# State mixer of an encoder: B and C tables stored as [group, channel], scan products and cross sum through PSUM

## The chip, the cores and the metric

The kernel runs on one core of one Trainium2 chip. The metric is device time in microseconds (us). Engines: TensorE (PE; its weight loads PEld), VectorE (DVE), ScalarE (ACT), GpSimd (POOL), SyncE (SP, which issues most DMAs). L498 is line 498 of the kernel before.

## The reference

Two layers over 1040 tokens of width 1024 (16 learned tokens and 1024 inputs). Layer 0 mixes tokens with a bidirectional diagonal complex state space, layer 1 with attention; after each comes a dense SwiGLU layer, and every sub-layer ends in a layer norm. Only the state mixer is touched. Cut to what matters, one direction of it is:

```
abr, abi = exp(lam * dt)                       # one complex factor for each of 64 groups x 64 states
bu  = einsum('blgc,gpc->blgp', u, Bbar)        # 16 channels of a group into 64 complex states
s_t = a * s_{t-1} + bu_t                       # along the 1040 tokens, forwards or in reverse
y   = einsum('blgp,gcp->blgc', Re s, c_re) - einsum('blgp,gcp->blgc', Im s, c_im)
```

The mixer adds both directions and d * u, applies GELU and a gate, and multiplies by an output matrix.

## The kernel before

The tokens are cut into 130 chunks (NK) of T = 8. Partitions 0 to 63 hold the 64 states of the forward direction, 64 to 127 those of the backward one, which is stored in reverse order of the chunks. The state mixer (`s5_phase`) has these stages; each engine takes its instructions in the order in which the code issues them.

Tables. `param_T` transposes the raw B and C parameters on TensorE, four channels to a PSUM bank, and ScalarE copies each bank into a table (L206). The table is laid out as [channel, re or im, group]: for a fixed group, channels lie 128 numbers apart, and 64 apart in the sums Hs and Cs.

G batches (`g_batch`, `x_batch`, 16 batches of four groups). VectorE multiplies B by powers of the factor: three products that read the tables (L335 to L337) and two sums of tiles just made (L338, L339); the k tiles are two deep. TensorE transposes the results (two banks), ScalarE copies them to W (L345), and TensorE multiplies them by the inputs U (four banks), which ScalarE copies into XS, the state of every chunk (L357). Batches 2 to 9 also take part of the input layout with them (one bank, L183 and L191). Beside this GpSimd makes power tables for C (`out_side`).

Scan (L478 to L503). 128 steps, one chunk each, all on VectorE. A step works on two halves of the 64 groups with six instructions: two products with the factor into TA (L494, 128 columns; the factor SB lies in PSUM), two sums of TA and the next chunk (L496, 64 columns), two cross sums (L498, 64 columns) that write the next state.

Written out by hand into the scan's loop stand other engines' instructions, at fixed steps: GpSimd's `e_batch` (five products or sums that make E from C, L386 to L390; the first four or five are issued before the scan), and for every batch `inside`: GpSimd's small dI (L424, L442, L443), TensorE's products of B and E (L433), ScalarE copies to Z (L439 to L441), eight DMAs from Z into M0 (L449), TensorE's products of M0 and U in two banks (L455), ScalarE copies back to U (L460). From step 66 on, `swap` turns the backward half of XS round, piece by piece: a copy to a PSUM bank (L467), and after the matching step two copies back (L470, L471).

Output. For all groups TensorE multiplies E by XS (L521), VectorE adds U (L523), and DMAs carry the result out. Then the gate and the dense layers follow. Just before L521, `late` starts the weight loads and conversions of the gate.

PSUM has eight banks; `bank()` hands out those of the pool `s5_ps` in turn, so a tile waits for the last user of the tile seven allocations before it.

Of the kernel before, what the change touches and what calls it, by code (L numbers as in the profile page):

```python
# [9 lines left out]
FP32 = mybir.dt.float32  # L10
# [3 lines left out]
ALU = mybir.AluOpType  # L14
PSUM = bass.MemoryType.PSUM
# [4 lines left out]
G = 64  # L20
# [5 lines left out]
CH = 16  # L26
T = 8
# [3 lines left out]
def bc(ap, dim, n):  # L31

    a = ap.unsqueeze(dim)
    shape = list(a.shape)
    shape[dim] = n
    return a.to_broadcast(shape)
# [77 lines left out]
def s5_phase(nc, tc, P, a, ident, acc, xres, ydram, late):  # L114

    V, A, PE, PO = nc.vector, nc.scalar, nc.tensor, nc.gpsimd
    ps = P("s5_ps", bufs=7, space=PSUM)

    psc = P("s5_psc", space=PSUM)

    def bank(name="b"):
        return ps.tile([128, 512], FP32, tag="b", name=name)

    def transpose(out, x):
        n = x.shape[0]
        PE.transpose(out, x, ident[:n, :n])

    U = Uv(acc)
    tab = P("s5_tab")
    tab2 = P("s5_tab2")  # L130
# [43 lines left out]
    for k in range(2):  # L174
        nc.sync.dma_start(out=XT[64 * k:64 * k + 64],
                          in_=a["x"][0, 1008 + T * k:1008 + T * k + T, :].rearrange("t (g c) -> g t c", c=CH))
# [16 lines left out]
    def x_tail():  # L193
        b = bank()
        transpose(b[:, :128], XT.rearrange("p t c -> p (t c)"))
        A.copy(out=U[:, :, 128:130], in_=b[:, :128].rearrange("p (k g) -> p g k", k=2))

    def param_T(x, raw):

        PT = tab.tile([128, CH, 2, G], FP32, name=x + "T")  # L200
        for h in range(4):
            b = bank()
            for c4 in range(4):
                c = 4 * h + c4
                transpose(b[:, c4 * 128:c4 * 128 + 128], raw[:, c::CH] if x == "b" else raw[:, c * 128:c * 128 + 128])
            A.copy(out=PT[:, 4 * h:4 * h + 4], in_=b.rearrange("p (c i g) -> p c i g", c=4, g=G))  # L206
        return PT[:, :, 0], PT[:, :, 1]

    load_x(2)
    raw_c = load_param("c")  # L210
# [37 lines left out]
        x_main(p, XG0[:, 4 * p:4 * p + 4])  # L248
    Br, Bi = param_T("b", raw_b)
    x_tail()  # L250
    Hs = tab2.tile([128, CH, G], FP32, name="Hs")
    PO.tensor_tensor(out=Hs, in0=Br, in1=Bi, op=ALU.add)
    AC = pc.tile([64, 4, 128], FP32, name="AC")
    cm, nr, sh, sn, t1, t2, rden = (t[n] for n in ("cm", "nr", "sh", "sn", "t1", "t2", "rden"))
# [17 lines left out]
    b = bank()  # L272
# [38 lines left out]
    Cr, Ci = param_T("c", raw_c)  # L311
    dsk = tab.tile([CH, G], FP32, name="dsk")
    b = bank()
    transpose(b[:CH, :G], dsr)
    A.copy(out=dsk, in_=b[:CH, :G])
    Cs = tab.tile([128, CH, G], FP32, name="Cs")

    SB = psc.tile([128, 512], FP32, name="SB")[:, :256].rearrange("p (j c g) -> p j c g", j=2, g=G)
    A.copy(out=SB[:, 0], in_=bc(PW[:, 0, 8], 1, 2))
    A.copy(out=SB[:, 1, 0], in_=PW[:, 1, 8])  # L320
    A.mul(SB[:, 1, 1], PW[:, 1, 8], -1.0)

# [6 lines left out]
    def g_batch(gb):  # L329
        gs = slice(NB * gb, NB * gb + NB)  # L330
        shp = [128, NB, T, CH]
        q_r, q_s, q_d = (bc(q[:, :, gs].rearrange("p s g -> p g s"), 3, CH) for q in G3)
        h_r, h_i, h_s = (bc(h[:, :, gs].rearrange("p c g -> p g c"), 2, T) for h in (Br, Bi, Hs))
        k1, k2, k3 = (gp.tile(shp, FP32, tag=f"k{i}", name=f"k{i}") for i in range(3))
        V.tensor_tensor(out=k1, in0=h_s, in1=q_r, op=ALU.mult)  # L335
        V.tensor_tensor(out=k2, in0=h_i, in1=q_s, op=ALU.mult)
        V.tensor_tensor(out=k3, in0=h_r, in1=q_d, op=ALU.mult)  # L337
        V.tensor_tensor(out=k2, in0=k1, in1=k2, op=ALU.subtract)  # L338
        V.tensor_tensor(out=k3, in0=k1, in1=k3, op=ALU.add)  # L339
        W = gp.tile([128, NB, 2, 128], FP32, tag="W", name="W")  # L340
        for c2, src in enumerate((k2, k3)):
            b = bank()
            for j in range(NB):
                transpose(b[:, j * 128:(j + 1) * 128], src[:, j].rearrange("p s c -> p (s c)"))
            A.copy(out=W[:, :, c2, :], in_=b.rearrange("p (g m) -> p g m", g=NB))  # L345
        return W
# [32 lines left out]
    def e_batch(gb):  # L379

        gs = slice(NB * gb, NB * gb + NB)
        g0 = NB * gb % (G // 2)
        q_r, q_s, q_d = (bc(q[:, :, gs].rearrange("p s g -> p g s"), 3, CH) for q in E3)
        c_r, c_i, c_s = (bc(c[:, :, gs].rearrange("p c g -> p g c"), 2, T) for c in (Cr, Ci, Cs))
        er, ei = (Eh[2 * gb // NG][:, i, g0:g0 + NB] for i in range(2))
        PO.tensor_tensor(out=ek, in0=c_s, in1=q_r, op=ALU.mult)  # L386
        PO.tensor_tensor(out=er, in0=c_i, in1=q_s, op=ALU.mult)
        PO.tensor_tensor(out=er, in0=ek, in1=er, op=ALU.subtract)
        PO.tensor_tensor(out=ei, in0=c_r, in1=q_d, op=ALU.mult)
        PO.tensor_tensor(out=ei, in0=ei, in1=ek, op=ALU.subtract)  # L390
# [3 lines left out]
    for gb in range(NG):  # L394
        p = 8 + gb - X_AT
# [20 lines left out]

    Eh[1] = P("s5_e1", side="right").tile([128, 2, G // 2, T, CH], FP32, name="E1")
    rp = P("s5_r")
    TA = rp.tile([128, 2, 2, 2, G // 2], FP32, name="TA")
    def inside(gb):  # L420

        gs = slice(NB * gb, NB * gb + NB)
        dI = rp.tile([CH, NB, CH], FP32, tag="dI", name="dI")
        PO.tensor_tensor(out=dI, in0=bc(ident[:CH, :CH], 1, NB), in1=bc(dsk[:, gs], 2, CH), op=ALU.mult)  # L424
        yield 2

        b = bank()
        for j in range(NB):
            g = NB * gb + j
            for c2, src in enumerate((Br, Bi)):  # L430
                for d in range(2):
                    r = slice(64 * d, 64 * d + 64)
                    PE.matmul(b[32 * d:32 * d + CH, j * 128:(j + 1) * 128], src[r, :, g],  # L433
                              E(c2, g)[r].rearrange("p s c -> p (s c)"), start=(c2 == 0), stop=(c2 == 1))
        yield 6
        Z = rp.tile([CH, NB, 2 * T - 1, CH], FP32, tag="Z", name="Z", bufs=2)
        bv = b[:64].rearrange("p (g s c) -> p g s c", g=NB, s=T)
        f0 = rp.tile([CH, NB, CH], FP32, tag="f0", name="f0")
        A.copy(out=f0, in_=bv[0:16, :, 0, :])  # L439
        A.copy(out=Z[:, :, 0:T, :], in_=bv[32:48])  # L440
        A.copy(out=Z[:, :, T:, :], in_=bv[0:16, :, 1:T, :])  # L441
        PO.tensor_tensor(out=dI, in0=dI, in1=f0, op=ALU.add)  # L442
        PO.tensor_tensor(out=Z[:, :, T - 1, :], in0=Z[:, :, T - 1, :], in1=dI, op=ALU.add)  # L443
        yield 8
        M0 = rp.tile([128, NB, 128], FP32, tag="M0", name="M0", bufs=2)
        Zf = Z.rearrange("p g s c -> p g (s c)")
        for t in range(T):
            o = (T - 1 - t) * CH
            nc.sync.dma_start(out=M0[CH * t:CH * t + CH], in_=Zf[:, :, o:o + 128])  # L449
        yield Y_AT  # L450
        banks = []
        for j0 in range(0, NB, 2):
            b = bank()
            for j in range(2):
                PE.matmul(b[:, j * NK:(j + 1) * NK], M0[:, j0 + j], U[:, NB * gb + j0 + j, :], start=True, stop=True)  # L455
            banks.append(b)
        yield Y_AT + 3
        for j0, b in zip(range(0, NB, 2), banks):
            g = NB * gb + j0
            A.copy(out=U[:, g:g + 2, :], in_=b[:, :2 * NK].rearrange("p (g k) -> p g k", g=2))  # L460
# [17 lines left out]
    for i in range(2, NK):  # L478
        for gb in range(NG):
            if i == 2 + int(E_PACE * (gb - EARLY)):  # L480
                e_batch(gb)
            l0 = 3 + int(L_PACE * gb)
            if i == l0:
                work[gb] = [inside(gb), l0]
        for gb in list(work):
            if i >= work[gb][1]:
                at = next(work[gb][0], None)
                if at is None:
                    del work[gb]
                else:  # L490
                    work[gb][1] = 3 + int(L_PACE * gb) + at
        st, nx = XS[:, i - 1], XS[:, i]
        for h, gs in enumerate(halves):
            V.tensor_tensor(out=TA[:, h], in0=SB[:, :, :, gs], in1=bc(st[:, :, gs], 1, 2), op=ALU.mult)  # L494
        for h, gs in enumerate(halves):
            V.tensor_tensor(out=TA[:, h, 0], in0=TA[:, h, 0], in1=nx[:, :, gs], op=ALU.add)  # L496
        for h, gs in enumerate(halves):
            V.tensor_tensor(out=nx[:, :, gs], in0=TA[:, h, 0], in1=TA[:, h, 1, ::-1], op=ALU.add)  # L498
        if sw and len(begun) < 2 and i > NK // 2:
            begun.append((sw[0][0], swap(*sw.pop(0))))  # L500
            next(begun[-1][1])
        while begun and NK - 1 - begun[0][0] <= i - 1:
            next(begun.pop(0)[1], None)  # L503
# [11 lines left out]
    for ft in range(KT):  # L515
        for g0 in range(8 * ft, 8 * ft + 8, 2):
            b = bank()
            for j in range(2):
                g = g0 + j
                for c2 in range(2):  # L520
# [3 lines left out]
                            in1=b[:, :2 * NK].rearrange("p (g k) -> p g k", g=2), op=ALU.add)  # L524
# [1052 lines left out]
```

## Time and profile before

| | us |
|---|---|
| median of 3 runs (lowest to highest) | 2938.03 (2931.74 to 2938.48) |
| the profiled execution | 2936.13 |
| its span | 2934.4 |
| TensorE busy in the span | 2656.4 (91%) |
| VectorE busy | 1651.7 (56%) |
| ScalarE busy | 1153.1 (39%) |
| GpSimd busy | 584.0 (20%) |

The shares are means over stages with different limits: in the page's 40 slices TensorE is at 5, 5, 4, 3 and 6 tenths in the first five (about 73 us each) and at 8 or more in nearly all the rest. So the state mixer is read by windows, and by the order of time of each engine. A row of the timeline has the start, the length, the engine, the line, the operation and the tiles; "x2" means two instructions of a kind in one row, whose length is that of both. A new VectorE instruction starts before the record of the one before it ends, so the distance of starts tells what an instruction takes of the engine.

### The profile page before, as it was taken

The page shows a single profiled execution, that of the slowest core. Times are in us where ns is not written, and L with a number is a line of the kernel's source. Part 1 is how long each engine was busy: PE and PEld are TensorE (multiplying, and loading weights), DVE is VectorE, ACT ScalarE, POOL GpSimd, SP SyncE. Part 2 cuts the span into 40 slices and gives each one's busy share as a digit, 9 for nine tenths or more (in the row PEclk, how much of TensorE's full clock was granted, in tenths as well). Part 3 has the DMA queues.
Part 4 walks back from the last instruction along what each step waited for, and adds up shares of the span by engine and source line. Part 5 has one row for each costly group of instructions (what it writes and reads, how often), then busy time and mean ns, then how long its engine had stood idle before and what let it go on. Part 6 is the DMA issues. An engine that isn't in the chain of part 4 may idle for free.

```text
span 2934.4 us, 43407 instructions
## 1 busy us (share of the span) xinstructions
PE 2656.4 (91%) x17277; PEld 2551.9 (87%) x17277; DVE 1651.7 (56%) x3270; ACT 1153.1 (39%) x2138; POOL 584.0 (20%) x544
## 2 busy tenths in 40 slices
PE   5543689999999999998998998999999999999997
PEld 4432689999999999997997887888999999999996
DVE  8999545573333333337867888887364333333334
ACT  5523353432222112125557777776332121211215
POOL 3983023230000000004204343432230000000002
PEclk8865799999999999998999999999999999999998
DMA  5110375221111111111301121111111111111101
GB/s 120 27 37 16 90 228 177 72 90 63 50 49 46 44 44 44 44 44 58 102 15 37 23 48 27 45 23 60 50 42 52 51 44 51 44 51 44 44 30 58
DMA packets 124837, 167.42 MB, mean 57 GB/s; under 512 B 13499, under 2 KB 104971, under 8 KB 124635
## 3 DMA queue, kind: packets, MB, share of 16 engines
q1 hardware_dynamic: 118203, 141.22, 17.0%
q0 software_dynamic: 5712, 21.30, 2.1%
q8 instruction: 136, 2.23, 0.3%
q10 hardware_dynamic: 720, 2.13, 0.2%
q14 instruction: 66, 0.54, 0.1%
HBM read 126.41 MB, written 21.23 MB: 50 GB/s over the span
## 4 chain that ended last, share of the span: by engine, by line
PE 74%; DVE 16%; ACT 3%; issue 3%; DMA 2%; POOL 1%; SPq 0%; ACTq 0%; DVEq 0%; POOLq 0%
PE bk L682 21%; PE bk L683 21%; PE bk L684 21%; PE pv L1094 4%; PE pt L1072 3%; DVE XS L498 3%; DVE TA L496 3%; DVE mx L1052 3%; DVE pl L1085 2%; PE b L521 2%; DVE TA L494 2%; ACT ph L1080 1%; ACT P L1056 1%; DVE acc L738 1%; PE bk L904 1%
## 5 line engine op out<-in xcount | busy, mean ns | idle before, releaser
L682 PE MATMUL bk<-Hh,unit 128*128 128x348 f32 (+1 forms) x2928 | 956.3, 327 | 9.8 <-ACT Hh L772 6.2
L683 PE MATMUL bk<-Hl,unit 128*128 128x348 f32 (+1 forms) x2928 | 945.4, 323 | 1.1 <-DVE Hl L776 1.0
L684 PE MATMUL bk<-Hh,unit 128*128 128x348 f32 (+1 forms) x2928 | 943.8, 322 | 0.0
L682 PEld LDWEIGHTS bk<-Hh,unit 128*128 128x128 f32 x2928 | 555.2, 190 | 15.1 <-ACT Hh L772 5.8
L683 PEld LDWEIGHTS bk<-Hl,unit 128*128 128x128 f32 x2928 | 554.9, 190 | 6.3 <-DVE Hl L776 2.0
L684 PEld LDWEIGHTS bk<-Hh,unit 128*128 128x128 f32 x2928 | 554.8, 189 | 0.0
L846 DVE TENSOR_TENSOR sg<-sg,bk 128x348 f32<-128x348 f32 x132 | 68.1, 516 | 631.3 <-PE bk L684 623.5
L711 POOL TENSOR_TENSOR lns<-lns,lnsq 128x348 f32<-128x348 f32 (+1 forms) x72 | 70.0, 981 | 1552.2 <-ACT lnsq L709 1551.1
L682 PE MATMUL bk<-gt,unit 128*128 128x348 f32 (+1 forms) x1056 | 340.3, 322 | 0.0
L684 PE MATMUL bk<-gt,unit 128*128 128x348 f32 (+1 forms) x1056 | 338.9, 321 | 0.0
L683 PE MATMUL bk<-gt,unit 128*128 128x348 f32 (+1 forms) x1056 | 338.2, 320 | 0.0
L869 DVE TENSOR_TENSOR acc<-acc,bk 128x348 f32<-128x348 f32 (+1 forms) x480 | 237.5, 513 | 112.7 <-PE bk L684 112.7
L848 ACT CAST gt<-sg 128x348 fp32r<-128x348 f32 x132 | 63.6, 482 | 489.1 <-DVE sg L846 489.1
L1072 PE MATMUL pt<-ident,P 128*116 128x128 f32 (+1 forms) x1188 | 181.7, 279 | 44.8 <-DVE pl L1085 40.5
L1085 DVE TENSOR_TENSOR pl<-pt,ph 116x512 fp32r<-116x512 f32 (+3 forms) x340 | 204.4, 619 | 15.1 <-ACT ph L1080 13.4
L1060 POOL TENSOR_SCALAR P<-P,l 128x1044 f32<-128x1044 f32 x132 | 149.8, 1147 | 292.5 <-PE pv L1094 167.7
L1072 PEld LDWEIGHTS pt<-ident,P 128*116 128x116 f32 (+1 forms) x1188 | 133.0, 136 | 81.1 <-issue 30.7
L683 PEld LDWEIGHTS bk<-gt,unit 128*128 128x128 f32 x1056 | 198.7, 188 | 0.5 <-issue 0.2
L682 PEld LDWEIGHTS bk<-gt,unit 128*128 128x128 f32 x1056 | 198.7, 188 | 0.5 <-issue 0.2
L684 PEld LDWEIGHTS bk<-gt,unit 128*128 128x128 f32 x1056 | 198.5, 188 | 0.0
L1080 ACT CAST ph<-pt 116x512 fp32r<-116x512 f32 (+3 forms) x340 | 168.9, 535 | 74.4 <-PE pt L1072 60.1
L597 ACT CAST unit<-raw 128x1024 fp32r<-128x1024 f32 x110 | 113.1, 1046 | 212.9 <-DMA raw<-in_ffn_w_up_dram 168.4
(285 smaller groups left out, 4123.1 us busy)
## 6 DMA issues: line engine op xcount, KB each, us to landing
raw<-in_ffn_w_gate_dram SPq DMA_DIRECT2D x44, 512.0 KB
raw<-in_ffn_w_up_dram SPq DMA_DIRECT2D x44, 512.0 KB
raw<-in_ffn_w_down_dram SPq DMA_DIRECT2D x44, 512.0 KB
y<-xdram SPq DMA_DIRECT2D x16, 520.0 KB
QA<-QH SPq DMA_DIRECT2D x30, 260.0 KB
raw<-in_attn_w_qkv_dram SPq DMA_DIRECT2D x14, 512.0 KB
xdram<-acc SPq DMA_DIRECT2D x32, 130.0 KB
xres<-xn POOLq DMA_DIRECT2D x8, 520.0 KB, 5.1
```

Of the source, the lines that this page charges most:

```text
L496: V.tensor_tensor(out=TA[:, h, 0], in0=TA[:, h, 0], in1=nx[:, :, gs], op=ALU.add)
L498: V.tensor_tensor(out=nx[:, :, gs], in0=TA[:, h, 0], in1=TA[:, h, 1, ::-1], op=ALU.add)
L597: A.copy(out=u[:, 0], in_=r)
L682: mm(out, wh, xh, start=(first and i == 0), stop=False)
L683: mm(out, wh, xl, start=False, stop=False)
L684: mm(out, wl, xh, start=False, stop=(last and i == n - 1))
L869: V.tensor_tensor(out=x, in0=x, in1=b, op=ALU.add)
L1060: PO.tensor_scalar(out=k.P, in0=k.P, scalar1=k.l, scalar2=1.0, op0=ALU.mult, op1=ALU.mult)
L1072: PE.transpose(b[:m, w * i + 128 * x:w * i + 128 * x + 128], u.P[x][:, KB_N * kt:KB_N * kt + m], self.ident)
L1080: A.copy(out=u.ph[s][:m, :w], in_=u.t[s][:m, :w])
L1085: V.tensor_tensor(out=u.pl[s][:m, :w], in0=u.t[s][:m, :w], in1=u.ph[s][:m, :w].bitcast(FP32), op=ALU.subtract)
L1094: PE.matmul(u.o[:, :u.w], VAs[u.j][:m, kt], (u.ph, u.pl)[x][s][:m, c:c + u.w], start=(kt == 0 and x == 0), stop=(kt == KBS - 1 and x == 1))
```

## The change

Three things are edited. The tables of B and C, and Hs and Cs, are laid out as [group, channel], so that the channels of a group are neighbours; ScalarE's copies in `param_T` now read their bank at a stride. The scan's product tile TA moves to PSUM, in a bank of its own apart from SB, and the sum of line 496 goes to a new SBUF tile TS, which line 498 adds to the other half of TA. For that bank the pool `s5_ps` has six banks in place of seven.

```diff
-    ps = P("s5_ps", bufs=7, space=PSUM)
+    ps = P("s5_ps", bufs=6, space=PSUM)
...
-        PT = tab.tile([128, CH, 2, G], FP32, name=x + "T")
+        PT = tab.tile([128, 2, G, CH], FP32, name=x + "T")
...
-            A.copy(out=PT[:, 4 * h:4 * h + 4], in_=b.rearrange("p (c i g) -> p c i g", c=4, g=G))
-        return PT[:, :, 0], PT[:, :, 1]
+            A.copy(out=PT[:, :, :, 4 * h:4 * h + 4], in_=b.rearrange("p (c i g) -> p i g c", c=4, g=G))
+        return PT[:, 0], PT[:, 1]
...
-    Hs = tab2.tile([128, CH, G], FP32, name="Hs")
+    Hs = tab2.tile([128, G, CH], FP32, name="Hs")
...
-    Cs = tab.tile([128, CH, G], FP32, name="Cs")
+    Cs = tab.tile([128, G, CH], FP32, name="Cs")
...
+    TA = psc.tile([128, 512], FP32, name="TA")[:, :256].rearrange("p (h j c g) -> p h j c g", h=2, j=2, c=2)
...
-        h_r, h_i, h_s = (bc(h[:, :, gs].rearrange("p c g -> p g c"), 2, T) for h in (Br, Bi, Hs))
+        h_r, h_i, h_s = (bc(h[:, gs], 2, T) for h in (Br, Bi, Hs))
...
-        c_r, c_i, c_s = (bc(c[:, :, gs].rearrange("p c g -> p g c"), 2, T) for c in (Cr, Ci, Cs))
+        c_r, c_i, c_s = (bc(c[:, gs], 2, T) for c in (Cr, Ci, Cs))
...
-    TA = rp.tile([128, 2, 2, 2, G // 2], FP32, name="TA")
+    TS = rp.tile([128, 2, 2, G // 2], FP32, name="TS")
...
-                    PE.matmul(b[32 * d:32 * d + CH, j * 128:(j + 1) * 128], src[r, :, g],
+                    PE.matmul(b[32 * d:32 * d + CH, j * 128:(j + 1) * 128], src[r, g],
...
-            V.tensor_tensor(out=TA[:, h, 0], in0=TA[:, h, 0], in1=nx[:, :, gs], op=ALU.add)
+            V.tensor_tensor(out=TS[:, h], in0=TA[:, h, 0], in1=nx[:, :, gs], op=ALU.add)
...
-            V.tensor_tensor(out=nx[:, :, gs], in0=TA[:, h, 0], in1=TA[:, h, 1, ::-1], op=ALU.add)
+            V.tensor_tensor(out=nx[:, :, gs], in0=TS[:, h], in1=TA[:, h, 1, ::-1], op=ALU.add)
```

## Rows read from the trace of the kernel before

**Rows 1.** Timeline of TensorE: the last products of M0, the first y matmuls.
```profile
305.04 2.07 PE L455 MATMUL b<-acc,M 128*128 128x130 f32 x8 [4.94 <-DMA M<-Z]
323.69 6.55 PE L521 MATMUL b<-XS,E 128*128 128x130 f32 x28 [16.59 <-ACT XS L471]
```

**Rows 2.** Windows of the G batches and the scan: busy us (instructions) by engine.
```profile
28.00:57.00 29.00, 18.24 (x111) 15.21 (x112) 28.97 (x21) 13.06 (x24) 21.10 (x11) 0.65 0.48 111
57.00:84.00 27.00, 23.05 (x270) 18.40 (x269) 27.00 (x32) 25.75 (x50) 7.52 (x1) 1.00 0.20 41
84.00:110.70 26.70, 18.97 (x243) 15.60 (x242) 26.70 (x30) 21.75 (x39) 26.70 (x1) 1.00 0.22 41
115.40:209.10 93.70, 42.49 (x423) 32.27 (x420) 93.10 (x157) 18.25 (x46) 89.18 (x93) 0.73 0.13 27
209.10:249.40 40.30, 4.04 (x35) 2.83 (x33) 40.30 (x259) 3.48 (x8) 0.00 (x0) 0.50 0.02 5
249.40:322.80 73.40, 26.21 (x184) 20.30 (x184) 73.40 (x354) 36.38 (x78) 24.97 (x32) 0.57 0.15 37
```

**Rows 3.** Timeline of VectorE in the scan, beside GpSimd (120) and alone (212).
```profile
120.30 0.48 DVE L494 TENSOR_TENSOR TA<-SB,XS 128x128 f32<-128x128 f32 x2
120.70 2.36 DVE L496 TENSOR_TENSOR TA<-TA,XS 128x64 f32<-128x64 f32 x2
122.98 1.42 DVE L498 TENSOR_TENSOR XS<-TA 128x64 f32<-128x64 f32 x2
...
212.65 0.48 DVE L494 TENSOR_TENSOR TA<-SB,XS 128x128 f32<-128x128 f32 x2
213.05 0.34 DVE L496 TENSOR_TENSOR TA<-TA,XS 128x64 f32<-128x64 f32 x2
...
213.59 0.48 DVE L494 TENSOR_TENSOR TA<-SB,XS 128x128 f32<-128x128 f32 x2
```

**Rows 4.** Timeline of GpSimd: the first E product, the last inside sum.
```profile
76.48 35.58 POOL L386 TENSOR_TENSOR ek<-Cs,E 128x512 f32<-128x512 f32 x1 [21.37 <-ACT E L307]
...
297.63 0.31 POOL L443 TENSOR_TENSOR Z<-Z,dI 16x64 f32<-16x64 f32 x1 [0.28 <-ACT Z L440]
```

**Rows 5.** Groups by line, GpSimd, 110 to 300 us: busy us, mean ns.
```profile
L387 POOL TENSOR_TENSOR E<-cT,E 128x512 f32<-128x512 f32 x16 | 21.8, 1363 | 0.0
...
L388 POOL TENSOR_TENSOR E<-ek,E 128x512 f32<-128x512 f32 x16 | 20.3, 1267 | 1.3
```

**Rows 6.** Timeline of ScalarE: the first swap, an inside copy, a swap's second part.
```profile
243.70 0.58 ACT L467 COPY b<-XS 64x512 f32<-64x512 f32 x1 [42.08 <-DVE XS L498]
...
308.54 0.65 ACT L460 COPY acc<-b 128x260 f32<-128x260 f32 x2
310.65 0.61 ACT L470 COPY XS<-XS 64x512 f32<-64x512 f32 x1 [1.46 <-DVE XS L498]
```

**Rows 7.** Timeline of VectorE: one G batch and the start of the next.
```profile
57.18 1.06 DVE L335 TENSOR_TENSOR k<-Hs,G 128x512 f32<-128x512 f32 x1
...
60.47 0.69 DVE L338 TENSOR_TENSOR k<-k,k 128x512 f32<-128x512 f32 x1
...
61.66 1.07 DVE L335 TENSOR_TENSOR k<-Hs,G 128x512 f32<-128x512 f32 x1
```

**Rows 8.** Timeline of VectorE: G sums while GpSimd makes its power tables.
```profile
37.21 1.71 DVE L338 TENSOR_TENSOR k<-k,k 128x512 f32<-128x512 f32 x1
38.84 1.75 DVE L339 TENSOR_TENSOR k<-k,k 128x512 f32<-128x512 f32 x1
```

**Rows 9.** Timeline of ScalarE: the copies of the B table, the copy after them.
```profile
15.43 2.06 ACT L206 COPY bT<-b 128x512 f32<-128x512 f32 x4
19.29 0.28 ACT L196 COPY acc<-b 128x128 f32<-128x128 f32 x1 [1.79 <-PE b L126]
```

**Rows 10.** Timeline of VectorE: a product, and the sum that needs it at once.
```profile
20.15 0.22 DVE L107 TENSOR_TENSOR w<-PW 128x64 f32<-128x64 f32 x1
20.41 0.23 DVE L108 TENSOR_TENSOR PW<-w,w 128x64 f32<-128x64 f32 x1
```

## The prediction

> **What bounds the kernel now.** I read the windows first. Behind the state mixer TensorE is busy in 8 tenths or more of nearly every slice and nothing there is edited, so what matters is when that part may begin: the y matmuls of line 521 start at 323.69, after TensorE sat idle 16.59 us, last for ScalarE's last swap copy [rows 1]. Before them lie two stages in which VectorE is busy for the whole window [rows 2]: the G batches (28 to 110.7) and the scan (115.4 to 322.8). The windows split the scan in three: while GpSimd is busy (89.18 of 93.70) VectorE gets 157 instructions through in 93.7 us, while GpSimd is idle 259 in 40.3 us. Six instructions are one step, so an undisturbed step is 40.3 / 259 x 6 = 0.93 to 0.94 us.
>
> The timeline says which instructions pay [rows 3]. Undisturbed, two of line 494 take 0.40 us from start to start (212.65 to 213.05), the two of 496 and the two of 498 take 0.54 together (213.05 to 213.59), 0.135 each. In a disturbed step line 494 still starts its successor after 0.40 (120.30 to 120.70), but two of 496 last 2.36 and two of 498 1.42. Line 494 reads SB from PSUM and one operand from SBUF; 496 and 498 read both from SBUF. So the wait belongs to the instruction with two SBUF operands while GpSimd reads SBUF. The other side shows it too: one GpSimd product, 1.36 us for its like [rows 5], lasted 35.58 us while VectorE ran G batches without a gap [rows 4].
>
> **Part by part.**
>
> *TA in PSUM.* After the change line 494 writes PSUM, 496 reads TA from PSUM and nx from SBUF, 498 reads TS from SBUF and TA from PSUM: none has two SBUF operands. I give all six the undisturbed times: 128 steps x 0.94 = 120 us, against 322.8 - 115.4 = 207.4 now: 87 us less for VectorE. What an added PSUM operand costs is not shown for 64 columns, nor a VectorE write to PSUM. Bounds: nothing, since 494, with a PSUM operand, takes 0.20 for 128 columns and 496 takes 0.135 for 64, and the 0.065 between them is no more than 64 columns at about 1.04 ns each, which leaves no surcharge for PSUM; below nothing has no row. The other end is one more fixed part (0.20 - 128 x 1.04 ns = 0.067) for each new access, four reads and two writes: 0.40 a step, 1.34 us. I take nothing, as 494 is the nearest row, and keep 1.34 (51 us) for the range.
> [...]
>
> *The work beside the scan.* VectorE waits for none of it, but the y matmuls wait for all of it, and it now becomes late. GpSimd makes sixteen E batches of five products, 3 x 1.36 + 2 x 1.27 = 6.6 us [rows 5], and three small ones per batch for the inside work, about 1 us (0.31 for the one at 297.63 [rows 4]): 16 x 7.6 = 122 us. Today it starts at 110.7 (76.48 + 35.58 - 1.36). Unhindered it would end at 233. Behind it comes the tail of the last batch: from its end (297.63 + 0.31) by the M0 loads to its matmuls at 305.04, 2.07 for these [rows 1], 0.65 for the copies [rows 6], 10 us; then the swaps queued behind on ScalarE. One is three copies of 0.58 to 0.61, 1.8 us [rows 6]; five come after the last inside copy: 9 us. So with G as it is the y matmuls start at about 252 and not at 115.4 + 120 + 1: a gain of 72 and not 87. ScalarE's 42.08 us wait for the scan at the first swap [rows 6] goes, because the scan is then ahead of the side work.
>
> *B and C tables as [group, channel].* In G, three products read them at a stride: 3.29 us (57.18 to 60.47), 1.10 each, where the two sums on contiguous tiles take 1.19 (to 61.66), 0.60 each [rows 7]; 4.48 us in all. The stride is the only thing the two kinds don't share apart from the broadcast of the other factor, so I take 0.60 to 0.65 for all, 3.1 us a batch; the other end is no change. The three products of an E batch would fall from 1.36 to 1.27: 5 us in all. VectorE's G batch at 3.1 is then below ScalarE's, 25.75 / 6 = 4.3 us [rows 2] for batches with x copies and an estimated 3.5 without (of the 21.75 us of six later ones [rows 2] some still is x copies). From the batches before 57 I take 6 us (some eight strided products each 0.4 to 0.5 less, the rest because GpSimd's part ends sooner); six batches at 4.3 for 4.48 give 1; six more at 3.5 for about 4.5 give 6. Alone: 12 to 13 us, the scan starts at 103.
>
> But VectorE now has gaps in G, since its k tiles are two deep, and GpSimd's 35.58 us wait ends at the first gap. It would be ready at about 70 (76.48 less the 6 to 7 us) and enter soon after, at 72. Its first five batches (25 products; what follows them waits for G's memory) then alternate with 25 G instructions: 1.63 us a pair while GpSimd's table products ran (37.21 to 38.84 [rows 8]), 1.36 + 0.60 = 1.96 at most: 41 to 49 us, to 113 to 121; four instructions are left (2.4), and 4.7 us lie between the last one and the first step (110.7 to 115.4): 120 to 128. I take 123. The side work is then ahead (five of sixteen done, end at about 118 + 11 x 7.4 = 200), and the scan sets the end: 123 + 120 + 1.2 = 244. With GpSimd kept out instead: 252 - 12.5 - 5 for the E products = 235 to 240. The two lie close because what one side gains at the shared read the other gives.
>
> *Costed at nothing.* The transposing copies of the B table read PSUM at a stride: they end at 17.5 and ScalarE then idles 1.79 us [rows 9]; above 0.45 us more per copy, each 0.1 would cost 0.4 us. The weight loads of line 433 become contiguous, but TensorE is busy 42.49 of 93.70 us there [rows 2]. Six banks for seven: a G batch takes two for W, four for XS and one for x, and the queue behind a waiting matmul is TensorE's own, 23.05 of 27 us busy; ScalarE goes on as long as one filled bank lies ahead of it. If that cover is gone, one copy of 0.6 us in 16 batches, 9 us. The w_glu loads stand behind the M0 loads on SP and move with them; their first use follows the last swap by a few matmul groups.
>
> **Sum.** 323.7 - 244.2 = 79.5 us off the span of 2934.4: 2854.9, with the 1.7 us around it (2936.13 profiled) 2856.6. The median of the runs is 1.9 above the profiled run: 2858 us.
>
> **Rivals.**
> 1. *The side work sets the end, or G gives nothing.* For: the sum above has it at 252 with G unchanged; hand-overs between GpSimd, TensorE, ScalarE and the loads could add 5. Against: 0.60 beside 1.10. Start at 250 to 257, gain 67 to 74: 2864 to 2871. Chance 0.2.
> 2. *PSUM has a price.* A step of 1.21 us (the four reads at 0.067) to 1.34 (the two writes too): 123 + 155 to 172 + 1.2 = 279 to 296, gain 28 to 44: 2894 to 2910. Against: line 494. Chance 0.1. [...]
> 3. *Slower: a PSUM result returns so late that the next pair waits for it.* Where one SBUF result is awaited by the very next instruction, 64 columns go from 0.14 to 0.26 us between starts (20.41 against the undisturbed 0.135) [rows 10]. If a TA write or read makes each of the six wait like that, a step is 4 x 0.26 + 2 x 0.33 = 1.70 us, the scan 218 us from 123 on, and the y matmuls start at 342: 18 us later, 2956. It decides from (323.7 - 123 - 1.2) / 128 = 1.56 us a step. Against: between a result and its use lies the other half's instruction, and a record of 0.21 us ends before the use at 0.27. Chance 0.04.
> 4. *The change doesn't do what it says*: one SBUF operand is enough to wait for GpSimd. Then only G moves, 0 to 12 us less: 2926 to 2938. Against: 494's 0.40 in the disturbed steps. Chance 0.04.
>
> **How the numbers follow.** The forecast, start of the y matmuls at 234 to 250, gain 74 to 90 (2848 to 2864), has 0.62. The range 2846 to 2886 holds it, rival 1 and the near half of what lies toward rival 2 (a price of half the bound); rivals 2 to 4 at full price are left out. Within 0.3% (about 9 us, what a measurement tells from no change) falls a part of rival 4: 0.02; slower is rival 3: 0.04; faster 0.94.
>
> **What would show it.** The six scan instructions at 0.20, 0.20 and four at 0.135 in every step, while GpSimd works, show the first part right; 1.2 us or more even when GpSimd is idle shows rival 2. Products of lines 335 to 337 at 0.6 show the layout right; the first E product ending at 72 to 75 and G instructions of 1.6 to 2 us behind it show GpSimd's early entry; an idle VectorE between scan end and the first y matmul of more than 2 us shows rival 1. Scan instructions above 0.5 us beside GpSimd would make the prediction wrong.

## The result, and the profile after

The changed kernel takes 2902.11 us (median of 4 runs, 2901.71 to 2904.21) against 2936.31 (4 runs, 2931.74 to 2938.48) for the kernel before on the same chip: ratio 0.9887, 95% interval 0.9870 to 0.9904. That is 34 us less; 80 were forecast, and the time lies above the range. The profiled execution took 2902.31 us, its span is 2900.4. From here on the lines of the changed kernel behind L317 are one higher than before: the scan's products are L495, its sums L497 and L499, the y matmuls L522.

Timeline of TensorE, changed kernel (start, length, what; in brackets the idle time before and what ended it), the row that answers to [rows 1]:

```profile
289.81 2.57 PE L522 MATMUL b<-XS,E 128*128 128x130 f32 x10 [25.83 <-ACT XS L472]
```

The y matmuls start 33.9 us earlier than before (323.69), the whole gain: from their start to the end of the span it is 2610.6 us, against 2610.7 before. They should have started at 244.2. So the 45.6 us that are missing were lost ahead of 289.81, and the windows say where (columns as in [rows 2]):

```profile
28.00:56.00 28.00, 25.64 (x291) 22.59 (x292) 27.97 (x47) 24.93 (x55) 22.58 (x1) 0.94 0.56 125
56.00:84.00 28.00, 15.92 (x182) 13.91 (x182) 25.13 (x16) 18.03 (x37) 27.32 (x18) 0.87 0.36 68
84.00:114.30 30.30, 18.55 (x154) 15.34 (x150) 30.30 (x21) 13.95 (x24) 28.96 (x19) 0.72 0.01 2
121.10:209.00 87.90, 37.44 (x414) 29.97 (x408) 80.95 (x402) 19.21 (x49) 54.05 (x70) 0.71 0.15 31
209.00:249.40 40.40, 25.09 (x200) 19.31 (x200) 37.23 (x186) 22.93 (x49) 21.53 (x30) 0.63 0.16 33
249.40:288.90 39.50, 4.54 (x16) 3.67 (x16) 36.40 (x181) 15.18 (x32) 0.62 (x2) 0.50 0.12 34
```

In the scan VectorE now gets through 402 instructions in 87.9 us with GpSimd busy for 54, and 181 in 39.5 with GpSimd idle: 0.219 and 0.218 us each. GpSimd no longer matters to it. But the undisturbed rate of before was 259 in 40.3, 0.156 each. And VectorE is not quite full: 36.40 of 39.50. It waits in every step, for something that is not GpSimd.

The timeline of VectorE shows it, beside GpSimd (122) and alone (262), as in [rows 3]:

```profile
122.14 0.63 DVE L495 TENSOR_TENSOR TA<-SB,XS 128x128 f32<-128x128 f32 x2
122.81 0.35 DVE L497 TENSOR_TENSOR TS<-TA,XS 128x64 f32<-128x64 f32 x2
123.08 0.34 DVE L499 TENSOR_TENSOR XS<-TS,TA 128x64 f32<-128x64 f32 x2
...
262.70 0.63 DVE L495 TENSOR_TENSOR TA<-SB,XS 128x128 f32<-128x128 f32 x2
263.37 0.35 DVE L497 TENSOR_TENSOR TS<-TA,XS 128x64 f32<-128x64 f32 x2
263.64 0.34 DVE L499 TENSOR_TENSOR XS<-TS,TA 128x64 f32<-128x64 f32 x2
264.02 0.63 DVE L495 TENSOR_TENSOR TA<-SB,XS 128x128 f32<-128x128 f32 x2
```

A step is 1.315 us (262.70 to 264.02), with GpSimd or without. The two products take 0.67 from start to start (262.70 to 263.37) where they took 0.40; the sums 0.27 and 0.38 where they took 0.27 each. By single instructions, in ns from one start to the next (the last of the six runs to the next step's first product): 333, 333, 142, 130, 128, 249; before: 201, 198, 133, 135, 135, 135. A product's record lasts 299 ns, so its successor starts 34 ns behind its end; before, a record lasted 278 ns and the successor started 77 ns ahead of its end.

The waits written into the two compiled programs name the reason. Each VectorE instruction of the scan counts up one counter when it is done, so an instruction that waits for the value 185 waits for number 185. For the six instructions of one step and the first two of the next (two products, two sums, two cross sums, two products):

```
before   number     186 187 188 189 190 191   192 193
         waits for  184 185 186 187 188 189   190 191
after    number     186 187 188 189 190 191   192 193
         waits for  185 186 187  -  188 189   191 192
```

Before, each waits for the one before the last. Now both products and the first sum wait for the instruction directly ahead of them (186, 187 and 188, and again 192 and 193); the second sum has no wait of its own. A half's product waits for the other half's, the first sum for the second half's product, the next step's first product for the second half's cross sum. None of these pairs touch the same numbers; all touch the same PSUM bank.

GpSimd, the rows that answer to [rows 4]:

```profile
33.42 24.82 POOL L369 TENSOR_TENSOR Cs<-cT 128x1024 f32<-128x1024 f32 x1 [12.88 <-ACT cT L206]
58.20 1.71 POOL L106 TENSOR_TENSOR w<-PW,acT 128x512 f32<-128x512 f32 x1
...
74.43 1.45 POOL L387 TENSOR_TENSOR ek<-Cs,E 128x512 f32<-128x512 f32 x1
75.83 1.56 POOL L388 TENSOR_TENSOR E<-cT,E 128x512 f32<-128x512 f32 x1
...
253.13 0.31 POOL L444 TENSOR_TENSOR Z<-Z,dI 16x64 f32<-16x64 f32 x1 [0.28 <-ACT Z L441]
```

The long wait has moved to an earlier product (Cs, 24.82 us), and the first E product is through at 75.9 instead of 112.1. Five of the sixteen E batches are done when G ends. In the groups by line from 121 to 235 us, beside [rows 5], the product that reads the C table takes 1.09 us, not 1.36; the sum is as before:

```profile
L389 POOL TENSOR_TENSOR E<-ek,E 128x512 f32<-128x512 f32 x11 | 13.9, 1268 | 0.9
...
L388 POOL TENSOR_TENSOR E<-cT,E 128x512 f32<-128x512 f32 x11 | 12.0, 1092 | 0.0
```

VectorE in G, one batch ahead of GpSimd's entry, as in [rows 7], and one behind it, as in [rows 8]:

```profile
28.23 0.69 DVE L336 TENSOR_TENSOR k<-Hs,G 128x512 f32<-128x512 f32 x1
28.84 0.69 DVE L337 TENSOR_TENSOR k<-bT,G 128x512 f32<-128x512 f32 x1
...
31.25 0.69 DVE L336 TENSOR_TENSOR k<-Hs,G 128x512 f32<-128x512 f32 x1
...
82.73 1.58 DVE L336 TENSOR_TENSOR k<-Hs,G 128x512 f32<-128x512 f32 x1
84.24 1.60 DVE L337 TENSOR_TENSOR k<-bT,G 128x512 f32<-128x512 f32 x1
...
112.62 1.75 DVE L340 TENSOR_TENSOR k<-k,k 128x512 f32<-128x512 f32 x1
```

Undisturbed, a batch is 3.02 us (28.23 to 31.25), against 4.48 in [rows 7] and 4.11 at the same place before (28.16 to 32.27); all five instructions take 0.60. Once GpSimd is in, each takes 1.51 to 1.68, 7.9 a batch, and G ends at 114.4, later than before (110.8). ScalarE's swaps, as in [rows 6], and its table copies, as in [rows 9] (the dependent pair of [rows 10] is not touched):

```profile
15.75 2.05 ACT L206 COPY bT<-b 128x512 f32<-128x512 f32 x4
...
203.65 0.58 ACT L468 COPY b<-XS 64x512 f32<-64x512 f32 x1 [30.08 <-DVE XS L499]
...
288.96 0.40 ACT L471 COPY XS<-XS 64x256 f32<-64x256 f32 x1 [4.05 <-DVE XS L499]
```

The first swap copy still waits 30 us for the scan, and the last one waits 4.05 us for it: the scan is last, not the work beside it. The transposing copies cost what the plain ones did.

### The profile page after: what moved, and what is told of

The parts are those of the page before. It is cut to its first block, busy times and chain, and to the rows that moved or that the text cites. A ratio compares the mean times of both kernels' runs of the same rounds, so it can differ in the third digit from the quotient of the medians.

```text
span 2900.4 us, 43401 instructions
## 1 busy us (share of the span) xinstructions
PE 2654.2 (92%) x17277; PEld 2555.6 (88%) x17277; DVE 1603.0 (55%) x3270; ACT 1149.0 (40%) x2138; POOL 565.5 (19%) x544
## 4 chain that ended last, share of the span: by engine, by line
PE 75%; DVE 14%; ACT 4%; issue 3%; POOL 2%; DMA 2%; SPq 0%; ACTq 0%; POOLq 0%; DVEq 0%
PE bk L683 21%; PE bk L684 21%; PE bk L685 21%; PE pv L1095 4%; PE pt L1073 3%; DVE TA L495 3%; DVE mx L1053 2%; DVE pl L1086 2%; PE b L522 2%; DVE TS L497 2%; ACT ph L1081 1%; DVE XS L499 1%; DVE acc L739 1%; POOL Cs L369 1%; DVE Hl L734 1%
```

## The experiments

Theory W: instructions of VectorE that touch one PSUM bank are put behind one another's end by a wait, whichever columns they use; the excess of 0.375 us a step is those three waits. Rival P: a PSUM operand has a price of its own (rival 2 of the prediction, 1.21 to 1.34 us a step). The six versions are compared with the kernel before on their chip: 2935.53 us for the first four, 2935.15 for the last two. The last three columns, in us, are from one profiled execution each (for tables only the fastest of its four runs, 2905.57).

| version | median us (runs) | ratio, 95% interval | G ends | scan ends | y matmuls start |
|---|---|---|---|---|---|
| the kernel before | 2936.31 (4) | | 110.8 | 322.8 | 323.69 |
| the changed kernel | 2902.11 (4) | 0.9887, 0.9870 to 0.9904 | 114.4 | 288.9 | 289.81 |
| two banks | 2853.65 (4) | 0.9718, 0.9702 to 0.9733 | 115.6 | 240.7 | 241.56 |
| full width, one bank | 2876.86 (5) | 0.9797, 0.9782 to 0.9813 | 114.9 | 264.3 | 265.18 |
| tables only | 2911.38 (4) | 0.9911, 0.9894 to 0.9929 | 113.7 | 294.6 | 295.45 |
| PSUM only | 2898.05 (4) | 0.9869, 0.9854 to 0.9885 | 111.9 | 285.5 | 286.42 |
| two banks, old tables | 2873.38 (5) | 0.9786, 0.9771 to 0.9802 | 112.2 | 235.9 | 260.85 |
| two banks, E held back | 2848.90 (4) | 0.9706, 0.9689 to 0.9722 | 90.2 | 213.9 | 233.26 |

**A bank for each half.** The changed kernel with the two halves of TA in a bank each.

```diff
-    ps = P("s5_ps", bufs=6, space=PSUM)
+    ps = P("s5_ps", bufs=5, space=PSUM)
...
-    TA = psc.tile([128, 512], FP32, name="TA")[:, :256].rearrange("p (h j c g) -> p h j c g", h=2, j=2, c=2)
+    TA = [psc.tile([128, 512], FP32, name=f"TA{h}")[:, :128].rearrange("p (j c g) -> p j c g", j=2, c=2) for h in range(2)]
...
```

> TA's two halves in a PSUM bank each (five banks left for the rotating pool), all else as in the changed kernel. Theory W (instructions that touch one PSUM bank are ordered one behind the other by a wait, so with both halves in one bank a product waits for the instruction just ahead of it): the waits go back to the instruction before the last, a step falls from 1.315 to 0.94 us, 128 x 0.375 = 48 us; the scan starts at 121 as in the changed kernel, the y matmuls at 121 + 120 + 1 = 242 to 245: 2854 to 2858 us. Rival P (a VectorE access to PSUM costs a fixed surcharge, whoever waits): step stays at 1.31, 2900 to 2905 us. If five banks are too few for the work beside the scan, VectorE is through at 242 and the y matmuls wait for ScalarE's swaps: 2860 to 2870.

Its scan on VectorE, while GpSimd works, and its first y matmuls:

```profile
130.52 0.49 DVE L495 TENSOR_TENSOR TA<-SB,XS 128x128 f32<-128x128 f32 x2
130.92 0.35 DVE L497 TENSOR_TENSOR TS<-TA,XS 128x64 f32<-128x64 f32 x2
131.18 0.34 DVE L499 TENSOR_TENSOR XS<-TS,TA 128x64 f32<-128x64 f32 x2
131.44 0.49 DVE L495 TENSOR_TENSOR TA<-SB,XS 128x128 f32<-128x128 f32 x2
```

```profile
241.56 50.81 PE L522 MATMUL b<-XS,E 128*128 128x130 f32 x227 [13.68 <-ACT XS L472]
```

A step takes 0.92 us with the same operands, the same sizes and one more bank; in its program each instruction again waits for the one before the last. So the price is not that of an access to PSUM: rival P falls, W stands. The time is 2853.65, where the prediction's sum had 2858.

**Full width.** One instruction for both halves, three a step, in one bank: every wait is now a true one.

```diff
-        for h, gs in enumerate(halves):
-            V.tensor_tensor(out=TA[:, h], in0=SB[:, :, :, gs], in1=bc(st[:, :, gs], 1, 2), op=ALU.mult)
...
+        V.tensor_tensor(out=TA, in0=SB, in1=bc(st, 1, 2), op=ALU.mult)
+        V.tensor_tensor(out=TS, in0=TA[:, 0], in1=nx, op=ALU.add)
+        V.tensor_tensor(out=nx, in0=TS, in1=TA[:, 1, ::-1], op=ALU.add)
```

> One bank for TA as in the changed kernel, but each step is three instructions over both halves (256, 128, 128 columns) in place of six. Theory W: each waits for the end of the one ahead, which the changed kernel's records time as 0.30 + 64 to 128 columns more at 1.04 ns + 0.034: 0.467 + 0.326 + 0.316 = 1.11 us a step, 26 us less than the changed kernel: 2875 to 2879 us. Rival P (a surcharge of 0.063 us for each of the instructions, 0.375 over six): 0.333 + 0.2 + 0.2 + 3 x 0.063 = 0.92 us, 51 us less: 2850 us. If the halves are there to hide something that W does not know, the step is above 1.3 us and it is slower than the changed kernel.

Timeline of VectorE:

```profile
130.72 0.43 DVE L494 TENSOR_TENSOR TA<-SB,XS 128x256 f32<-128x256 f32 x1
131.19 0.29 DVE L495 TENSOR_TENSOR TS<-TA,XS 128x128 f32<-128x128 f32 x1
131.52 0.29 DVE L496 TENSOR_TENSOR XS<-TS,TA 128x128 f32<-128x128 f32 x1
131.84 0.43 DVE L494 TENSOR_TENSOR TA<-SB,XS 128x256 f32<-128x256 f32 x1
```

Where a wait for the instruction directly ahead is a true one, the next starts 0.03 to 0.04 us after its end (131.19 is 0.04 after 130.72 + 0.43), the distance found in the changed kernel between halves that share nothing but the bank. Tiles in SBUF show the same distance behind such a wait [rows 10]: 20.41 is 0.04 after 20.15 + 0.22. So the wait alone accounts for the excess. And the second L497 of the changed kernel, which reads the bank directly behind the first and has no wait, follows it after 0.142 us (0.131 with two banks): a read directly behind a read of the same bank came 0.011 us later. Whether a write would be slowed by the bank itself, without the wait, no run shows. Three dependent instructions at 1.11 us a step beat six half-ordered ones at 1.315.

**Each part alone.** The tables with the old TA in SBUF and seven banks, and TA in PSUM with the old tables.

```diff
-    TA = psc.tile([128, 512], FP32, name="TA")[:, :256].rearrange("p (h j c g) -> p h j c g", h=2, j=2, c=2)
...
+    TA = rp.tile([128, 2, 2, 2, G // 2], FP32, name="TA")
...
```

> The tables as [group, channel] alone; TA in SBUF and seven banks as before. The scan starts at 121 as in the changed kernel, with five of the sixteen E batches done. If the loss of the scan before (207.4 - 120 = 87 us for sixteen E batches, 5.5 each) goes with the E batches that still lie beside it: eleven times 4.8 to 5.5, scan 173 to 180 us, y matmuls at 295 to 303: 2908 to 2915 us, so most of the measured 34 us comes from GpSimd's early entry into G, and TA in one bank adds only 6 to 13. Rival: the scan's time does not depend on how many E batches lie beside it, the tables then cost the 6 us by which the scan starts later: 2942 us.

```diff
-        PT = tab.tile([128, 2, G, CH], FP32, name=x + "T")
+        PT = tab.tile([128, CH, 2, G], FP32, name=x + "T")
...
```

> TA in one PSUM bank and six banks, with the old tables. G ends as before, scan from 115.4; step 1.315 (both W and P), 168 us, y matmuls at 284 to 286, 4 to 6 us before those of the changed kernel: 2896 to 2898 us. So beside TA in PSUM the tables cost a few us. Rival: the E batches, all beside or behind the scan now, end late (GpSimd until 233, tail of 19 us, 252): still before 284, so no change of the number; if the strided G batch costs more with six banks, the scan starts at 118 to 125 and it is no faster than the changed kernel.

Tables only, the first E product on GpSimd and a scan step on VectorE; then PSUM only, the first E product and a scan step:

```profile
71.94 1.43 POOL L386 TENSOR_TENSOR ek<-Cs,E 128x512 f32<-128x512 f32 x1
```

```profile
129.12 2.34 DVE L498 TENSOR_TENSOR XS<-TA 128x64 f32<-128x64 f32 x2
131.38 0.47 DVE L494 TENSOR_TENSOR TA<-SB,XS 128x128 f32<-128x128 f32 x2
131.78 1.29 DVE L496 TENSOR_TENSOR TA<-TA,XS 128x64 f32<-128x64 f32 x2
```

```profile
77.62 35.50 POOL L387 TENSOR_TENSOR ek<-Cs,E 128x512 f32<-128x512 f32 x1 [22.56 <-ACT E L307]
```

```profile
130.20 0.63 DVE L495 TENSOR_TENSOR TA<-SB,XS 128x128 f32<-128x128 f32 x2
130.87 0.36 DVE L497 TENSOR_TENSOR TS<-TA,XS 128x64 f32<-128x64 f32 x2
131.14 0.34 DVE L499 TENSOR_TENSOR XS<-TS,TA 128x64 f32<-128x64 f32 x2
131.52 0.63 DVE L495 TENSOR_TENSOR TA<-SB,XS 128x128 f32<-128x128 f32 x2
```

Both times came as expected. The tables alone save 24 us, without a shorter G (113.7): GpSimd enters G at 72, five E batches are done before the scan, and the scan, which still waits for GpSimd, lasts 176 us instead of 207. TA in one bank alone saves 37 us. Together they save 34: in PSUM the scan no longer cares how many E batches are left (a step is 1.32 us with none done ahead, 1.31 with five), so the tables lose what they were worth. In the two traces they still have a price, a G that ends 2.5 us later and y matmuls that start 3.4 us later; the intervals of the two times overlap.

**Two banks, old tables.** The counterpart: the tables' worth once the scan is fast.

```diff
-        PT = tab.tile([128, 2, G, CH], FP32, name=x + "T")
+        PT = tab.tile([128, CH, 2, G], FP32, name=x + "T")
...
```

> The scan of the two-bank version (each half of TA in a bank of its own) beside the old tables of B and C, which are read with a stride. Theory (the wait on the instruction ahead in the same bank was the whole excess, and the side work becomes the bound once the tables go back): G ends at about 111 us and the scan's first step at 115, as before the change; 128 steps of 0.95 us end it at 236 to 237 us. GpSimd starts its 16 E batches at about 111 us with products of up to 1.36 us, 16 x 7.6 = 122, so 233, and the tail and the swaps put the y matmuls at 252 to 257 us: total about 2864 to 2869 us. Rival (the contiguous tables bring nothing beyond the scan, their products are short without contention even with the stride): E ends by 218 us, the scan sets the end, y matmuls at 237.5 us, total about 2849 us.

The last E products on GpSimd, and the y matmuls:

```profile
231.14 1.38 POOL L390 TENSOR_TENSOR E<-cT,E 128x512 f32<-128x512 f32 x1
232.60 1.27 POOL L391 TENSOR_TENSOR E<-E,ek 128x512 f32<-128x512 f32 x1
...
241.92 0.31 POOL L444 TENSOR_TENSOR Z<-Z,dI 16x64 f32<-16x64 f32 x1 [1.92 <-ACT Z L441]
```

```profile
260.85 57.19 PE L522 MATMUL b<-XS,E 128*128 128x130 f32 x256 [6.51 <-ACT XS L472]
```

The scan ends at 235.9 as expected, the E batches at 233.9, and the y matmuls come 25 us behind the scan: the side work sets the end. The tables are then worth 20 us (2873.38 to 2853.65; the intervals lie apart). The expected start, 252 to 257, was 4 to 9 us too early: from the last E product to the y matmuls it takes 27.0 us, not 19, as the last inside sum ends 8.4 us behind the last E product (242.23 against 233.87).

**Two banks, E held back.** The first four E batches are issued behind G instead of beside it.

```diff
-    ek = tab.tile([128, NB, T, CH], FP32, name="ek")
...
-            for b in range(EARLY):
-                e_batch(b)
...
+    ek = rp.tile([128, NB, T, CH], FP32, name="ek")
+    for b in range(EARLY):
+        e_batch(b)
...
```

> The two-bank version with GpSimd's E batches held back until G has ended; the same instructions, only their order changes. Theory (G is slow behind 56 us only because GpSimd's products alternate with it at the shared read): the remaining G batches take 3.0 to 3.5 us each, G ends at about 91 us, the scan's first step is at 97 to 100 us and its end at 217 to 220 us; GpSimd needs 16 x 6.9 = 110 us from 91, so about 201, and with the tail the y matmuls start at 219 to 223 us, about 20 us ahead of the two-bank version: total about 2832 us. Rival (what one side gains at the shared read the other gives back, E's later start then sets the end): 3 to 8 us gained, total 2846 to 2851 us.

VectorE where GpSimd's power tables end and in the last G batch, GpSimd's first E product, and the y matmuls:

```profile
73.35 1.76 DVE L340 TENSOR_TENSOR k<-k,k 128x512 f32<-128x512 f32 x1
75.04 0.68 DVE L336 TENSOR_TENSOR k<-Hs,G 128x512 f32<-128x512 f32 x1
75.64 0.68 DVE L337 TENSOR_TENSOR k<-bT,G 128x512 f32<-128x512 f32 x1
...
89.49 0.69 DVE L340 TENSOR_TENSOR k<-k,k 128x512 f32<-128x512 f32 x1
```

```profile
95.15 1.10 POOL L386 TENSOR_TENSOR ek<-Cs,E 128x512 f32<-128x512 f32 x1 [20.59 <-PE b L356]
```

```profile
233.26 57.21 PE L522 MATMUL b<-XS,E 128*128 128x130 f32 x256 [6.51 <-ACT XS L472]
```

The theory is right about G: with GpSimd idle an instruction falls from 1.69 to 0.60 us at once, G ends at 90.2 and the scan at 213.9, 27 us earlier than with two banks alone. Its total is wrong. The last E product ends at 206.4 (201 expected), the y matmuls start 26.8 behind it, and the side work is last by 19 us. Of 27 us, 8 reach the y matmuls, and the time, 2848.90, is the rival's. The intervals of this version and of the two-bank one overlap.

## Why the prediction was wrong

**The step that failed** is the sentence on TA in PSUM, "I give all six the undisturbed times". A step takes 1.315 us, not 0.94: 128 x 0.375 = 48 us, against 45.6 missing at the y matmuls (the scan began 1.9 us earlier than forecast). With a bank for each half, and so with the step that the sentence took, the y matmuls start at 241.56 for a forecast of 244.2: the rest of the sum held. The prediction took TA as a tile with two independent halves, which it is in SBUF, where every scan instruction waits for the one before the last; in one bank the halves are ordered one behind another, and the gap that hides each result, the other half's instruction, became a wait on it (behind a product the next instruction starts 34 ns after the end of its record, before 77 ns ahead of it). The argument against rival 3, "between a result and its use lies the other half's instruction", is true of the data and not of the bank. The two 0.33 of that rival are the products' 333 ns as measured; of its four 0.26 one came, the 249 ns from the last cross sum to the next step's first product.

**Rival 2** gave 2894 to 2910 and holds the time, but by the wrong mechanism: with two banks the four sums read PSUM as often and take 0.13 us each. The sign set for it, 1.2 us or more with GpSimd idle, came, but it can't tell a price of the access from a wait. The 1.04 ns a column in its bound are an estimate from [rows 3] and [rows 7]: 0.60 us for a sum of 512 columns less 0.135 for one of 64, over 448 columns. The waits on the instruction directly ahead stand between instructions of one engine; whether they are needed there no run shows.

**GpSimd's hold on the scan** went as predicted: every step takes 1.31 to 1.32 us, with and without GpSimd, and rival 4 falls.

**G and the early entry** came out in numbers, in part by luck: 0.60 for each product, GpSimd's first E product in G (it ends at 75.9; 72 to 75 was forecast), 1.5 to 1.7 us an instruction after that, first step at 121.1 where 123 was taken. The way there was another. GpSimd's part did not end sooner: its Cs product was held until 58.2, and the power tables ran behind it, inside G, up to 74.4. In return G went undisturbed for nine batches, from 28.23 to 55.33, where the kernel before made four from 28.16 to 57.18. The two misses cancel. "Alone: 12 to 13 us, the scan starts at 103" was low: with E held back it starts at 95.7.

**The side work** did not set the end of the changed kernel, so rival 1 did not come. Its sizes: with G unchanged 252 was forecast, 260.85 came (two banks, old tables); with GpSimd kept out 235 to 240, 233.26 came (two banks, E held back). The tail behind the last E product was 8 us too short, the E products shorter than the 1.27 assumed.

**Costed at nothing**, the transposing copies cost nothing [rows 9]. Fewer banks in the pool may have a small price: the first sum of the scan starts at 116.48 with seven and 117.71 with six on the old tables, at 119.30 with seven and 121.49 with six on the new ones. These are single traces, and TA's move to PSUM is not separated from the pool in them.

## What to carry to other kernels

In programs whose waits go by bank, as these do (a step took 1.315 us with both halves of TA in one bank, 0.92 with a bank each), halves that are meant to overlap each need a PSUM bank of their own: look at what each instruction waits for in the compiled program, since a wait can follow the bank and not the bytes. Two gains from one shared wait need not add; ask of each what it is worth after the other. A stage that is made faster hands the end to the next chain, so work out that chain's tail from its last product on, with its hand-overs.

## What was not expected of the hardware

GpSimd's product of 1024 columns lasted 24.82 us while VectorE issued instructions with two SBUF operands without a gap, and one of 512 columns lasted 35.50 us in the PSUM-only version; once inside, the two engines alternate, about 1.6 us each. Which of the two goes first is not explained. In the changed kernel the Cs product got in where VectorE first left a gap (0.09 us ahead of 56.02; the G product issued there lasted 2.76 us). But in the kernel before the same product got in at once, between strided G products that followed each other without a gap:

```profile
33.64 2.82 POOL L368 TENSOR_TENSOR Cs<-cT 128x1024 f32<-128x1024 f32 x1 [13.41 <-ACT cT L206]
```

The G product issued at 34.21 then lasted 3.08 us. Yet the first E product of that kernel waited 35.58 us beside instructions of the same kind [rows 4]. Why that is so stays open.
